# The output projection's operand splits, queued one by one behind the weight splits of the running pair

## The chip, the cores and the metric

The kernel runs on one core of one Trainium2 chip. The metric is the device time of one execution, in microseconds (us), from a launch to its end; lower is better. The engines are TensorE (PE in the rows), VectorE (DVE), ScalarE (ACT), GpSimd (POOL) and SyncE (SP), which here only issues DMAs. Each works its own queue in order and waits on semaphores for the others.

## What is computed

One layer of a hybrid decoder trunk on x of 1024 x 1024 float32: an RMSNorm, one combined input projection, three causal token mixers beside each other (differential attention a, sliding-window attention b, forgetting attention c), a gate and an up-projection for each, a merge by sigmoid gates, an output projection with w_o, a residual add and a last RMSNorm.

```
h = rms_norm(x, norm_gain[l], RMS_EPS)
proj = jnp.einsum('bsd,de->bse', h, w_in[l])
...
merged = gates[:, :, 0] * ua + gates[:, :, 1] * ub + gates[:, :, 2] * uc
x = x + jnp.einsum('bsd,de->bse', merged, w_o[l])
...
return rms_norm(x, final_gain, RMS_EPS)
```

## The kernel before

A float32 product is made of three matmuls on a reduced float32 type: each operand is split into a high half (a cast, `hi`) and a low half (the source less the high half, `lo`), and `mm3` (L106) adds hi x hi, hi x lo and lo x hi in PSUM for each block of 128 rows of the contraction. `split` (L98) makes the two halves: with `act` set the cast runs on ACT (L101), and the subtraction runs on POOL (L104). `operand` (L145) splits a weight tile of 128 x 512 elements into `w_hi` and `w_lo`, which have four buffers each (`NW`); so a weight cast waits until PE has read the buffer's tile of four operands earlier.

The stages follow each other: the norm and the v columns; then the pair stage of this change; then attention with fillers on PE; then the up-projections; then the output projection.

The pair stage (the loop over `tiles`, two by two) makes 40 column tiles of the input projection for q, k and the gates. Two tiles at a time go through `strassen` (L158), which turns the 2 x 2 block product into 7 products instead of 8, each of 12 matmuls of 512 columns. Its weight operands are, in the order in which PE takes them: a11, s2, a12, s3, s1, s4, a22. Those with s are sums and differences of the four weight tiles, made on DVE by `comb` (L165, tile `w_sf`); the others are the loaded tiles (`w_st`, five buffers). In code, a11, a12 and s2 are split before the first result is yielded, s3 and s1 before the second, s4 before the third and a22 before the last. A result is scaled and split (`qk_hi`, `qk_lo`) or made a gate (`sg`) and stored to DRAM by SP.

The output projection at the kernel's end is a Strassen product too, and its seven w_o operands are made during the pair stage by `prepare` (L456). For each of four blocks k it loads four tiles of w_o (`ws`, four buffers; the load is ordered behind the last w_st load), takes four differences of them on DVE (L471, L472, L478, L481) and calls `put` (L447) seven times. A put casts its source on ACT to `pwh`, subtracts on POOL to `pwl` (both from one ring of `NPW` = 3 buffers) and stores both halves to the DRAM tensor `wod` through SP. From the second pair on, the loop takes one step of `prepare` at the first and at the second result of each pair: 8 steps a block, one of them the loads, 28 puts in all.

The order on each engine isn't that of the code. A scheduler arranges the instructions from their dependencies and a simulated timeline, and takes what it holds ready; nothing ties the puts to a place but their sources and buffers. `tc.issue_after(ins)` adds such a tie: instructions in its block that run on the engine of `ins` are queued behind it there. It is an order and no semaphore.

Of the kernel before, what the change touches and what calls it, by code (L numbers as in the profile page):

```python
# [9 lines left out]
F32 = mybir.dt.float32  # L10
F32R = mybir.dt.float32r
AF = mybir.ActivationFunctionType
ALU = mybir.AluOpType
# [7 lines left out]
NB = S // P  # L21
# [14 lines left out]
LAG, AHEAD, TVLAG = 2, 3, 1  # L36
# [13 lines left out]
def hybrid_block_kernel(ctx, tc, x, norm_gain, w_in, b_forget, lambda_q1, lambda_k1, lambda_q2, lambda_k2,  # L50
                        subln_gain, sinks, w_up_a, w_up_b, w_up_c, w_o, final_gain, out):
    nc = tc.nc
    x = x[0]
    out = out[0]
# [43 lines left out]
    def split(src, hi, lo, act=False, eng=nc.gpsimd):  # L98

        if act:  # L100
            nc.scalar.copy(hi, src)  # L101
        else:
            nc.gpsimd.tensor_scalar(out=hi, in0=src, scalar1=1.0, scalar2=1.0, op0=ALU.mult, op1=ALU.mult)
        return eng.tensor_tensor(lo, src, hi.bitcast(F32), ALU.subtract)  # L104

    def mm3(ps, w, r, start=True, stop=True, n=4):  # L106

# [26 lines left out]

    behind = [None]

    def load_st(src):
        st = wp.tile([P, 4, P], F32, name="w_st", bufs=NST)
        behind[0] = nc.sync.dma_start(st, src)
        return st  # L140

    def load_half(col0, i):
        return load_st(w_in[:, 4 * i:4 * i + 4, col0:col0 + P])

    def operand(st, act=False):  # L145
        wh = wp.tile([P, 4, P], F32R, name="w_hi", bufs=NW)
        wl = wp.tile([P, 4, P], F32R, name="w_lo", bufs=NW)
        split(st, wh, wl, act)
        return wh, wl

    def direct_tile(col0, psum, act=False):
# [64 lines left out]
    with tc.tile_pool(name="blk", bufs=8) as blk, \  # L216
# [6 lines left out]
        with tc.tile_pool(name="xp", bufs=2) as xp:  # L223

            last = {}
# [56 lines left out]
            def load_vw(ch, dma=nc.sync):  # L282

                n = 392 if ch == 0 else 384
                w = []
                if ch == 0:
                    fc = xp.tile([P, 8, 8], F32, name="fc", bufs=1)
                for i in range(2):
                    wh = blk.tile([P, 4, n], F32R, name=f"vw_h{ch}{i}", tag="blk", padded_shape=[P, 4, 512])
                    wl = blk.tile([P, 4, n], F32R, name=f"vw_l{ch}{i}", tag="blk", padded_shape=[P, 4, 512])  # L290
                    (c0, n0), (c1, n1) = v_cols[ch]
                    for k0, nk, o, c, cn in ((0, 4, 0, c0, n0), (0, 2, n0, c1, n1), (2, 2, n0, c1, n1)):
                        ws = wp.tile([P, nk, cn], F32, name=f"vw_s{ch}", tag="w_st", bufs=NST)
                        dma.dma_start(ws, w_in[:, 4 * i + k0:4 * i + k0 + nk, c:c + cn])
                        last["lo"] = split(ws, wh[:, k0:k0 + nk, o:o + cn], wl[:, k0:k0 + nk, o:o + cn], True)
                    w.append((wh, wl))
                if ch == 0:
                    nc.sync.dma_start(fc, w_in[:, :, FC:FC + 8])
                    for i in range(2):
                        split(fc[:, 4 * i:4 * i + 4, :], w[i][0][:, :, 384:392], w[i][1][:, :, 384:392], True)  # L300
                return w, n
# [114 lines left out]
        with tc.tile_pool(name="qkp", bufs=2, reuse_waits="tile") as qkp:  # L416
# [32 lines left out]
            def put(dst, k, src):  # L449

                hi, lo = (qkp.tile([P, 512], F32R, name=f"pw{t}", tag="pw", bufs=NPW) for t in "hl")
                split(src, hi, lo, True)
                for t, v in enumerate((hi, lo)):
                    nc.sync.dma_start(dst[t, :, k, :], v.bitcast(F32))

# [42 lines left out]
            for n in range(0, len(tiles), 2):  # L498
                first = ExitStack()
# [41 lines left out]
    def gate_tiles(br):  # L541
        yg[br] = [[hp_.tile([P, 4, 512], F32R, name=f"yg_{br}{c}{t}", tag="h", bufs=8) for t in range(2)]
                  for c in range(2)]
# [29 lines left out]
    with tc.tile_pool(name="at", bufs=2, reuse_waits="tile") as at, \  # L573
# [14 lines left out]
        def fill(n):  # L588
            owed[0] += n
            while owed[0] >= 1:  # L590
                owed[0] -= 1
                if left[0] > cur["keep"]:
                    left[0] -= 1
                    next(filler)
# [11 lines left out]
        def load_q(row, m):  # L606
            return load_rows(row, m, (0, 1))

        def load_k(row, m):
            return [load_rows(row, m, (t, t)) for t in range(2)]  # L610

        def load_v(unit):

            v = at.tile([P, NB, 2 * P], F32R, name="v")
            nc.sync.dma_start(v.bitcast(F32), vd[:, unit, :].rearrange("(kb p) e -> p kb e", p=P))
            return v
# [254 lines left out]
        def load_b(u, kv):  # L871
            if kv == 0:
                vb["v"] = load_v(0)
            r = slice(20 * P + 64 * kv, 20 * P + 64 * kv + 64)
            u["k"] = []
            for t in range(2):
                tg = ("e", NE) if kv and t else ("f", NF)
                k = at.tile([P, S], F32R, name=f"kb{kv}{t}", tag=tg[0], bufs=tg[1])
                for d in range(2):
                    nc.sync.dma_start(k[64 * d:64 * d + 64, :].bitcast(F32), qd[t, r, :])  # L880
                u["k"].append(k)
            u["q"] = [load_q(16 + 2 * kv + t, m) for t in range(2) for m in range(2)]
# [3 lines left out]
        def load_c(u, hp, hh):  # L886
            if hh == 0:
                vc[hp] = load_v(1 + hp)
            u["v"] = vc[hp]
            u["q"] = load_q(hp, hh)  # L890
            u["k"] = load_k(4 + hp, hh)

        def load_a(u, h):
            u["v"] = load_v(5 + h)
            u["q"], u["k"] = [None, None], [None, None]
            for m in range(2):
                u["q"][m] = load_q(8 + h, m)
                u["k"][m] = load_k(12 + h, m)

        parts = []  # L900
        for kv in range(2):
            u = {}
            parts += [((lambda u=u, kv=kv: load_b(u, kv)) if i == 0 else None, "b", part_b(u, kv, i)) for i in range(NB)]
        for hp in range(4):
            for hh in range(2):
                u = {}
                parts += [((lambda u=u, hp=hp, hh=hh: load_c(u, hp, hh)) if g == 3 else None, "c", part_c(u, hp, hh, g))
                          for g in (3, 2, 1, 0)]
        for h in range(4):
            u = {}  # L910
            parts += [((lambda u=u, h=h: load_a(u, h)) if g == 3 else None, "a", part_a(u, h, g)) for g in (3, 2, 1, 0)]

        rate = {"b": FILL_B, "c": FILL_C, "a": FILL_A}
        pending_v = []
        ahead = 0
# [8 lines left out]
        def tick(c):  # L924
            clock[0] += c
            for e in list(later):
                if e[0] <= clock[0]:
                    later.remove(e)
                    e[1]()
        gq = [gb[0][0]] + [f for n in range(8) for f in ([gb[n + 1][0]] if n < 7 else []) + [gb[n][1]]]  # L930
        for n in range(len(parts) + LAG):
            if "free" in cur:
                if "b" not in yg:
                    gate_tiles("b")
                for f in gq[:GPART]:
                    f()
                del gq[:GPART]

            while ahead < min(n + AHEAD + 1, len(parts)):
                if parts[ahead][0]:  # L940
                    parts[ahead][0]()
                if ahead >= len(parts):
                    break
                ahead += 1
            if n == 0:
                fill(FILL_0)
                parts[0][2][3]()
            if n + 1 < len(parts):
                parts[n + 1][2][3]()
            sa = list(parts[n][2][0]) if n < len(parts) else []  # L950
            tv = []
            if n >= LAG:
                _, ta, va, _ = parts[n - LAG][2]
                for t, v in zip(ta, va):
                    tv.append(t)
                    pending_v.append(v)
                    if len(pending_v) > TVLAG:
                        tv.append(pending_v.pop(0))
            if n == len(parts) + LAG - 1:
                tv += pending_v  # L960
            kind = parts[min(n, len(parts) - 1)][1]
            cs, ct = sum(c for c, _ in sa), sum(c for c, _ in tv)
            ps_, pt_ = 0.0, 0.0
            while sa or tv:
                if sa and (not tv or (ps_ + 0.5 * sa[0][0]) * ct <= (pt_ + 0.5 * tv[0][0]) * cs):
                    c, f = sa.pop(0)
                    ps_ += c
                else:
                    c, f = tv.pop(0)
                    pt_ += c  # L970
                f()
                if n < len(parts):
                    fill(c * rate[kind] / 0.65)
                else:
                    cur["keep"] = 0
                    fill(c * FILL_Z / 0.65)
                tick(c * (1 + rate[kind]))
# [4 lines left out]
    with tc.tile_pool(name="st", bufs=2, reuse_waits="tile") as st, \  # L982
# [90 lines left out]
        for br, nxt in ("bc", "ca", "a "):  # L1073
            if nxt != " ":
                gate_tiles(nxt)
            for d in range(NK):
                n = UPS.index((br, d))
# [11 lines left out]
        for sb in range(NB // 2):  # L1089
# [8 lines left out]
            for j, c, u in strassen(*halves, wo, psum3,  # L1098
# [4 lines left out]
                if (j, c) != (1, 0):  # L1103
                    nc.vector.tensor_tensor(t, u, t, ALU.add)
                    u, t = t, u
# [40 lines left out]
```

## Time and profile before

| what | us |
|---|---|
| median of 3 runs (lowest, highest) | 1203.62 (1195.36, 1210.67) |
| the profiled execution, device time | 1201.41 |
| its span, first to last instruction | 1199.3 |
| busy in the span: PE | 1155.8 |
| DVE | 798.9 |
| POOL | 688.9 |
| ACT | 591.9 |

The mean granted clock of TensorE is 0.984 of its upper level. The device time holds 2.1 us outside of the span. Busy shares are averages over stages with different limits, and a matmul's row is longer than its share of PE, since matmuls overlap in it: the pace of PE is read from start to start.

### The profile page before, as it was taken

What the parts mean: (1) busy time and instruction counts of PE and PEld (TensorE: products, weight loads), DVE (VectorE), ACT (ScalarE), POOL (GpSimd) and SP (SyncE); (2) the same over time, 40 slices, a digit from 0 to 9 for tenths busy, and PEclk for the clock granted to TensorE, in tenths of its full rate; (3) what the DMA queues carried; (4) which work ended last, traced back from release to release, by engine and by line L of the source; (5) the groups of instructions that cost most, each with busy time, mean ns of one, the idle gap of its engine ahead of it and who ended that gap; (6) DMA issues with size and microseconds to landing.
All of it is one profiled execution on the core that took longest, in us unless ns stands there. A gap on an engine that the chain in (4) does not pass through costs nothing. (4 is left out here: it accounts for less than half of the span.)

```text
span 1199.3 us, 18793 instructions
## 1 busy us (share of the span) xinstructions
PE 1155.8 (96%) x5787; PEld 977.3 (81%) x5787; DVE 798.9 (67%) x1655; ACT 591.9 (49%) x1255; POOL 688.9 (57%) x684
## 2 busy tenths in 40 slices
PE   7999999999999999999999999999998999989997
PEld 6999878878778788887888888888877778878885
DVE  7667786766775774321887766767766835564897
ACT  6432334333443443332886666667876842334433
POOL 5056585665754754454555666665767632377652
PEclk8999999999999999999999999999999999999999
DMA  7442386675854643338945465456567359897332
GB/s 242 159 154 80 112 283 201 216 246 158 257 192 138 221 132 106 114 97 244 272 131 173 145 195 176 130 174 174 171 209 221 122 169 325 270 333 299 141 119 92
DMA packets 184531, 221.70 MB, mean 185 GB/s; under 512 B 16280, under 2 KB 116712, under 8 KB 182640
## 3 DMA queue, kind: packets, MB, share of 16 engines
q1 hardware_dynamic: 184288, 219.99, 58.2%
q8 instruction: 46, 0.75, 0.3%
q10 hardware_dynamic: 144, 0.52, 0.1%
q14 instruction: 53, 0.43, 0.1%
HBM read 144.89 MB, written 75.56 MB: 184 GB/s over the span
## 5 line engine op out<-in xcount | busy, mean ns | idle before, releaser
L104 POOL TENSOR_TENSOR w_lo<-w_st,w_hi 128x512 fp32r<-128x512 f32 x130 | 175.4, 1352 | 109.5 <-ACT w_hi L101 99.0
L104 POOL TENSOR_TENSOR w_lo<-w_sf,w_hi 128x512 fp32r<-128x512 f32 x96 | 137.8, 1440 | 107.4 <-ACT w_hi L101 100.6
L111 PE MATMUL pm<-t,w_lo 128*128 128x512 f32 x320 | 128.7, 402 | 5.4 <-POOL w_lo L104 5.4
L109 PE MATMUL pm<-t,w_hi 128*128 128x512 f32 x320 | 128.5, 402 | 2.5 <-ACT w_hi L101 2.5
L110 PE MATMUL pm<-t,w_hi 128*128 128x512 f32 x320 | 127.6, 399 | 0.0
L625 PE MATMUL sc<-qk 128*128 128x512 f32 (+2 forms) x384 | 102.4, 358 | 4.4 <-DVE m L645 3.8
L101 ACT CAST w_hi<-w_sf 128x512 fp32r<-128x512 f32 x96 | 58.9, 616 | 57.5 <-PE pm L110 51.4
L678 DVE TENSOR_TENSOR pt<-tp,pt 128x512 fp32r<-128x512 f32 x102 | 70.1, 687 | 23.5 <-ACT pt L677 22.7
L101 ACT CAST w_hi<-w_st 128x512 fp32r<-128x512 f32 x86 | 52.4, 617 | 62.0 <-PE pm L110 51.1
L111 PEld LDWEIGHTS pm<-t,w_lo 128*128 128x128 f32 x320 | 61.2, 191 | 21.5 <-POOL w_lo L104 7.1
L625 PEld LDWEIGHTS sc<-qk 128*128 128x128 f32 x384 | 64.9, 190 | 16.3 <-DVE m L645 6.8
L109 PEld LDWEIGHTS pm<-t,w_hi 128*128 128x128 f32 x320 | 61.2, 191 | 17.7 <-ACT w_hi L101 3.7
L110 PEld LDWEIGHTS pm<-t,w_hi 128*128 128x128 f32 x320 | 61.4, 192 | 14.5
L677 ACT CAST pt<-tp 128x512 fp32r<-128x512 f32 x102 | 59.4, 583 | 20.1 <-PE tp L671 18.8
L167 DVE TENSOR_TENSOR w_sf<-w_st 128x512 f32<-128x512 f32 x40 | 43.7, 1093 | 36.0 <-DMA w_st<-in_w_in_dram 21.8
L659 POOL TENSOR_SCALAR e_c<-e_c,r 128x1024 f32<-128x1024 f32 (+3 forms) x64 | 47.9, 748 | 24.5 <-DVE r L653 20.1
L651 ACT ACTIVATE e_c<-e_c,m 128x1024 f32<-128x1024 f32 (+3 forms) x64 | 49.9, 780 | 16.0 <-DVE m L645 15.1
L704 PE MATMUL y<-pt,v 128*128 128x256 f32 x336 | 55.4, 290 | 2.1 <-DVE pt L678 1.8
L651 ACT ACTIVATE e_a<-e_a,m 128x896 f32<-128x896 f32 (+7 forms) x64 | 49.6, 776 | 14.9 <-DVE m L645 14.4
L835 POOL TENSOR_TENSOR e_a<-e_a,e_a 128x896 f32<-128x896 f32 (+7 forms) x32 | 47.6, 1490 | 15.3 <-ACT e_a L834 15.1
L704 PEld LDWEIGHTS y<-pt,v 128*128 128x128 f32 x336 | 48.0, 189 | 6.8 <-DVE pt L678 3.2
L104 POOL TENSOR_TENSOR pwl<-ws,pwh 128x512 fp32r<-128x512 f32 x28 | 40.7, 1455 | 19.9 <-ACT pwh L101 14.2
(299 smaller groups left out, 3467.5 us busy)
## 6 DMA issues: line engine op xcount, KB each, us to landing
w_st<-in_w_in_dram SPq DMA_DIRECT2D x126, 256.0 KB, 3.3
qk<-qd SPq DMA_DIRECT2D x224, 128.0 KB, 3.0
wo<-wod SPq DMA_DIRECT2D x14, 1024.0 KB, 9.3
row<-gmd SPq DMA_DIRECT2D x48, 256.0 KB, 5.1
qd<-qk_hi SPq DMA_DIRECT2D x42, 256.0 KB, 4.2
qd<-qk_lo SPq DMA_DIRECT2D x42, 256.0 KB, 3.8
vd<-vt SPq DMA_DIRECT2D x24, 384.0 KB, 2.3
v<-vd SPq DMA_DIRECT2D x9, 1024.0 KB, 8.2
```

What stands on the lines that cost most here:

```text
L101: nc.scalar.copy(hi, src)
L104: return eng.tensor_tensor(lo, src, hi.bitcast(F32), ALU.subtract)
L109: nc.tensor.matmul(ps, w[0][:, k, :], r[0][:, k, :], start=start and k == 0, stop=False)
L110: nc.tensor.matmul(ps, w[0][:, k, :], r[1][:, k, :], start=False, stop=False)
L111: nc.tensor.matmul(ps, w[1][:, k, :], r[0][:, k, :], start=False, stop=stop and k == n - 1)
L625: nc.tensor.matmul(ps[:, :n], q, kk[t][c][:, o:o + n], start=t == 0, stop=t == 1)
L651: nc.scalar.activation(e[:, :L], e[:, :L], AF.Exp, bias=m2, scale=-1.0, accum_out=den)
L659: nc.gpsimd.tensor_scalar(out=e, in0=e, scalar1=r, scalar2=1.0, op0=ALU.mult, op1=ALU.mult)
L677: nc.scalar.copy(pt[:, 0, a:], tp[:, a:])
L678: nc.vector.tensor_tensor(pt[:, 1, a:], tp[:, a:], pt[:, 0, a:].bitcast(F32), ALU.subtract)
L704: nc.tensor.matmul(y[:, :256], l_, r_, start=t == 0 and n == 0, stop=last and n == len(mms) - 1)
L835: nc.gpsimd.tensor_tensor(e1[:, :L], e1[:, :L], e2[:, :L], ALU.add)
```

## The change

The cast and the subtraction of a put, until now made by `split`, are written out in `put`, and each is ordered behind its counterpart of the weight operand that was split last in the code before it: the cast behind that operand's cast on ACT, the subtraction behind its subtraction on POOL. For this, `split` returns both instructions and `operand` keeps them in `parts`. (A list that was called `parts` in the attention stage is renamed `units`, which is left out here.)

```diff
     def split(src, hi, lo, act=False, eng=nc.gpsimd):

         if act:
-            nc.scalar.copy(hi, src)
+            first = nc.scalar.copy(hi, src)
         else:
-            nc.gpsimd.tensor_scalar(out=hi, in0=src, scalar1=1.0, scalar2=1.0, op0=ALU.mult, op1=ALU.mult)
-        return eng.tensor_tensor(lo, src, hi.bitcast(F32), ALU.subtract)
+            first = nc.gpsimd.tensor_scalar(out=hi, in0=src, scalar1=1.0, scalar2=1.0, op0=ALU.mult, op1=ALU.mult)
+        return first, eng.tensor_tensor(lo, src, hi.bitcast(F32), ALU.subtract)
...
+    parts = [None, None]
...
     def operand(st, act=False):
         wh = wp.tile([P, 4, P], F32R, name="w_hi", bufs=NW)
         wl = wp.tile([P, 4, P], F32R, name="w_lo", bufs=NW)
-        split(st, wh, wl, act)
+        parts[:] = split(st, wh, wl, act)
         return wh, wl
...
             def put(dst, k, src):

                 hi, lo = (qkp.tile([P, 512], F32R, name=f"pw{t}", tag="pw", bufs=NPW) for t in "hl")
-                split(src, hi, lo, True)
+                with tc.issue_after(parts[0].ins):
+                    nc.scalar.copy(hi, src)
+                with tc.issue_after(parts[1].ins):
+                    nc.gpsimd.tensor_tensor(lo, src, hi.bitcast(F32), ALU.subtract)
                 for t, v in enumerate((hi, lo)):
                     nc.sync.dma_start(dst[t, :, k, :], v.bitcast(F32))
```

The first place is POOL's queue at the first puts. Operands of the first pair are w_lo_1490 to w_lo_1598 (1574 is its s4, 1598 its a22), those of the second begin with w_lo_1630 (a11); 1661 is its s2, 1727 its s1. Before:

```order
L104 TENSOR_TENSOR w_lo_1548<-w_sf_1476,w_hi_1547 128x512
L104 TENSOR_TENSOR pwl_1751<-ws_1698,pwh_1750 128x512
L104 TENSOR_TENSOR w_lo_1574<-w_sf_1482,w_hi_1573 128x512
L104 TENSOR_TENSOR w_lo_1598<-w_st_1455,w_hi_1597 128x512
L104 TENSOR_TENSOR pwl_1886<-ws_1702,pwh_1885 128x512
L104 TENSOR_TENSOR w_lo_1630<-w_st_1620,w_hi_1629 128x512
L104 TENSOR_TENSOR pwl_1936<-ws_1704,pwh_1935 128x512
L104 TENSOR_TENSOR w_lo_1656<-w_st_1622,w_hi_1655 128x512
L104 TENSOR_TENSOR pwl_2069<-ws_1698,pwh_2068 128x512
L104 TENSOR_TENSOR w_lo_1661<-w_sf_1649,w_hi_1660 128x512
L104 TENSOR_TENSOR pwl_2120<-ws_1700,pwh_2119 128x512
L104 TENSOR_TENSOR w_lo_1708<-w_sf_1651,w_hi_1707 128x512
```

The same queue now, from the second pair's s1 to the third pair's s4:

```order
L104 TENSOR_TENSOR w_lo_1727<-w_sf_1647,w_hi_1726 128x512
L457 TENSOR_TENSOR pwl_1751<-ws_1698,pwh_1750 128x512
L104 TENSOR_TENSOR w_lo_1759<-w_sf_1653,w_hi_1758 128x512
L104 TENSOR_TENSOR w_lo_1783<-w_st_1626,w_hi_1782 128x512
L104 TENSOR_TENSOR w_lo_1815<-w_st_1805,w_hi_1814 128x512
L104 TENSOR_TENSOR w_lo_1841<-w_st_1807,w_hi_1840 128x512
L104 TENSOR_TENSOR w_lo_1846<-w_sf_1834,w_hi_1845 128x512
L457 TENSOR_TENSOR pwl_1886<-ws_1702,pwh_1885 128x512
L104 TENSOR_TENSOR w_lo_1893<-w_sf_1836,w_hi_1892 128x512
L104 TENSOR_TENSOR w_lo_1912<-w_sf_1832,w_hi_1911 128x512
L457 TENSOR_TENSOR pwl_1936<-ws_1704,pwh_1935 128x512
L104 TENSOR_TENSOR w_lo_1944<-w_sf_1838,w_hi_1943 128x512
```

The first put (pwl_1751) has moved from the first pair's s4 to behind the second pair's s1, and the next two stand behind s2 and s1 of the third pair, where five puts stood among seven weights. This goes on at two puts a pair.

The second place is ACT's queue at the same puts. Before:

```order
L101 CAST pwh_1750<-ws_1698 128x512
L101 CAST w_hi_1573<-w_sf_1482 128x512
L101 CAST pwh_1885<-ws_1702 128x512
L101 CAST w_hi_1597<-w_st_1455 128x512
L101 CAST w_hi_1629<-w_st_1620 128x512
L421 ACTIVATE qk_hi_1521<-u_1474 128x512
L101 CAST pwh_1935<-ws_1704 128x512
L101 CAST w_hi_1655<-w_st_1622 128x512
L101 CAST pwh_2068<-ws_1698 128x512
L421 ACTIVATE qk_hi_1565<-u_1563 128x512
```

And now, around the puts behind s2 (w_hi_1845) and s1 (w_hi_1911) of the third pair:

```order
L101 CAST w_hi_1845<-w_sf_1834 128x512
L455 CAST pwh_1885<-ws_1702 128x512
L423 ACTIVATE qk_hi_1775<-u_1676 128x512
L101 CAST w_hi_1892<-w_sf_1836 128x512
L423 ACTIVATE qk_hi_1799<-u_1723 128x512
L101 CAST w_hi_1911<-w_sf_1832 128x512
L455 CAST pwh_1935<-ws_1704 128x512
L174 COPY u_1830<-pm_1813 128x512
L101 CAST w_hi_1943<-w_sf_1838 128x512
```

A put's cast now has two to three weight casts between it and the next, where two followed each other with one weight cast between them. PE's queue is the same but for two places where two matmuls of a12's product stand a few rows later; the stages behind the pair stage are the same on all engines.

## Rows read from the trace of the kernel before

**Rows 1.** The page, part 1: busy time of each engine.

```profile
PE 1155.8 (96%) x5787; PEld 977.3 (81%) x5787; DVE 798.9 (67%) x1655; ACT 591.9 (49%) x1255; POOL 688.9 (57%) x684
```

**Rows 2.** Busy time by stretch: stretch, length, busy us (x instructions) by engine, PEclk, DMA.

```profile
190.00:230.00 40.00, 40.00 (x175) 32.52 (x174) 26.91 (x34) 17.70 (x30) 22.03 (x16) 1.00 0.63 201
...
470.00:510.00 40.00, 40.00 (x175) 32.52 (x174) 15.53 (x23) 14.77 (x25) 18.59 (x15) 1.00 0.38 106
```

**Rows 3.** Waits of PE from 150 to 430 us: total, times, longest.

```profile
PE pm L111 <- POOL w_lo L104: 5.4, 4, 2.3
PE pm L109 <- ACT w_hi L101: 1.8, 2, 0.9
```

**Rows 4.** Timeline of PE at four places: start us, us, instruction, [idle before <-releaser].

```profile
164.28 0.40 PE L109 MATMUL pm<-h10h,w_hi 128*128 128x512 f32 x1
167.00 0.62 PE L111 MATMUL pm<-t,w_lo 128*128 128x512 f32 x1 [2.32 <-POOL w_lo L104]
...
170.75 0.39 PE L111 MATMUL pm<-t,w_lo 128*128 128x512 f32 x1
...
245.31 0.39 PE L111 MATMUL pm<-h00h,w_lo 128*128 128x512 f32 x1
...
249.16 0.80 PE L111 MATMUL pm<-t,w_lo 128*128 128x512 f32 x1 [1.15 <-POOL w_lo L104]
...
252.67 0.39 PE L110 MATMUL pm<-t,w_hi 128*128 128x512 f32 x1
...
327.00 0.39 PE L111 MATMUL pm<-h00h,w_lo 128*128 128x512 f32 x1
...
334.60 0.39 PE L111 MATMUL pm<-t,w_lo 128*128 128x512 f32 x1
...
409.40 0.40 PE L109 MATMUL pm<-h10h,w_hi 128*128 128x512 f32 x1
410.56 0.50 PE L111 MATMUL pm<-t,w_lo 128*128 128x512 f32 x1 [0.76 <-POOL w_lo L104]
410.89 0.39 PE L109 MATMUL pm<-t,w_hi 128*128 128x512 f32 x1
```

**Rows 5.** Busy time by stretch, around the first of these places.

```profile
164.00:171.00 7.00, 4.68 (x14) 3.34 (x14) 6.26 (x7) 1.71 (x4) 5.51 (x4) 0.76 1.00 327
```

**Rows 6.** Timeline of POOL at the first of these places.

```profile
163.90 1.38 POOL L104 TENSOR_TENSOR pwl<-ws,pwh 128x512 fp32r<-128x512 f32 x1 [0.30 <-PE pm L110]
165.24 1.71 POOL L104 TENSOR_TENSOR w_lo<-w_sf,w_hi 128x512 fp32r<-128x512 f32 x1
```

**Rows 7.** What ended ACT's idle time before the puts' casts: us, times.

```profile
  DMA ws<-in_w_o_dram: 13.0, 6
...
  DMA wod<-pwl: 9.3, 7
```

**Rows 8.** Timeline of POOL in a pair without puts: s2, s3, s1, s4.

```profile
463.33 1.29 POOL L104 TENSOR_TENSOR w_lo<-w_sf,w_hi 128x512 fp32r<-128x512 f32 x1 [1.46 <-ACT w_hi L101]
466.12 1.30 POOL L104 TENSOR_TENSOR w_lo<-w_sf,w_hi 128x512 fp32r<-128x512 f32 x1 [1.50 <-ACT w_hi L101]
468.86 1.29 POOL L104 TENSOR_TENSOR w_lo<-w_sf,w_hi 128x512 fp32r<-128x512 f32 x1 [1.44 <-ACT w_hi L101]
471.86 1.30 POOL L104 TENSOR_TENSOR w_lo<-w_sf,w_hi 128x512 fp32r<-128x512 f32 x1 [1.71 <-ACT w_hi L101]
```

**Rows 9.** Timeline of PE in that pair: first matmul of s3's and s4's product.

```profile
473.68 0.40 PE L109 MATMUL pm<-t,w_hi 128*128 128x512 f32 x1
...
479.27 0.39 PE L109 MATMUL pm<-h11h,w_hi 128*128 128x512 f32 x1
```

**Rows 10.** The puts' subtractions by tile: ns min/median/max, first and last start; landing.

```profile
L104 POOL TENSOR_TENSOR pwl<-ws,pwh x28: 1280/1306/1832, 152.1 to 411.0; 128x512 fp32r<-128x512 f32 x28
...
DMA to landing us min/median/max: 2.8/3.8/5.0
```

**Rows 11.** DVE's subtractions on w_o tiles, one of four lines.

```profile
L471 DVE TENSOR_TENSOR ws<-ws x4: 675/1774/1783, 154.0 to 391.6; 128x512 f32<-128x512 f32 x4
```

More of the change, by code (lines that the diff above doesn't have):

```diff
@@ L294, in load_vw @@
                         dma.dma_start(ws, w_in[:, 4 * i + k0:4 * i + k0 + nk, c:c + cn])
-                        last["lo"] = split(ws, wh[:, k0:k0 + nk, o:o + cn], wl[:, k0:k0 + nk, o:o + cn], True)
+                        last["lo"] = split(ws, wh[:, k0:k0 + nk, o:o + cn], wl[:, k0:k0 + nk, o:o + cn], True)[1]
                     w.append((wh, wl))
@@ L898, in load_a @@
                 u["k"][m] = load_k(12 + h, m)
-        parts = []
+        units = []
         for kv in range(2):
             u = {}
-            parts += [((lambda u=u, kv=kv: load_b(u, kv)) if i == 0 else None, "b", part_b(u, kv, i)) for i in range(NB)]
+            units += [((lambda u=u, kv=kv: load_b(u, kv)) if i == 0 else None, "b", part_b(u, kv, i)) for i in range(NB)]
         for hp in range(4):
@@ L906, in hybrid_block_kernel @@
                 u = {}
-                parts += [((lambda u=u, hp=hp, hh=hh: load_c(u, hp, hh)) if g == 3 else None, "c", part_c(u, hp, hh, g))
+                units += [((lambda u=u, hp=hp, hh=hh: load_c(u, hp, hh)) if g == 3 else None, "c", part_c(u, hp, hh, g))
                           for g in (3, 2, 1, 0)]
@@ L910, in hybrid_block_kernel @@
             u = {}
-            parts += [((lambda u=u, h=h: load_a(u, h)) if g == 3 else None, "a", part_a(u, h, g)) for g in (3, 2, 1, 0)]
+            units += [((lambda u=u, h=h: load_a(u, h)) if g == 3 else None, "a", part_a(u, h, g)) for g in (3, 2, 1, 0)]
         rate = {"b": FILL_B, "c": FILL_C, "a": FILL_A}
@@ L930, in hybrid_block_kernel @@
         gq = [gb[0][0]] + [f for n in range(8) for f in ([gb[n + 1][0]] if n < 7 else []) + [gb[n][1]]]
-        for n in range(len(parts) + LAG):
+        for n in range(len(units) + LAG):
             if "free" in cur:
@@ L937, in hybrid_block_kernel @@
                 del gq[:GPART]
[L939 to L942, printed above, removed]
+            while ahead < min(n + AHEAD + 1, len(units)):
+                if units[ahead][0]:
+                    units[ahead][0]()
+                if ahead >= len(units):
                     break
@@ L946, in hybrid_block_kernel @@
                 fill(FILL_0)
[L947 to L950, printed above, removed]
+                units[0][2][3]()
+            if n + 1 < len(units):
+                units[n + 1][2][3]()
+            sa = list(units[n][2][0]) if n < len(units) else []
             tv = []
             if n >= LAG:
-                _, ta, va, _ = parts[n - LAG][2]
+                _, ta, va, _ = units[n - LAG][2]
                 for t, v in zip(ta, va):
@@ L958, in hybrid_block_kernel @@
                         tv.append(pending_v.pop(0))
-            if n == len(parts) + LAG - 1:
+            if n == len(units) + LAG - 1:
                 tv += pending_v
-            kind = parts[min(n, len(parts) - 1)][1]
+            kind = units[min(n, len(units) - 1)][1]
             cs, ct = sum(c for c, _ in sa), sum(c for c, _ in tv)
@@ L971, in hybrid_block_kernel @@
                 f()
-                if n < len(parts):
+                if n < len(units):
                     fill(c * rate[kind] / 0.65)
```

## The prediction

> **What bounds the kernel now.** I read the page first. TensorE (PE) is busy 1155.8 of the span's 1199.3 us [rows 1], so a change pays only where PE stands still or runs slower than it can. The change touches the stage that makes the q, k and gate tiles in pairs, roughly 140 to 515 us, so the second view is the busy time by stretch in that stage. In two stretches without any put of the output projection (190 to 230 and 470 to 510) PE is busy 40.00 of 40.00 us at a granted clock of 1.00, that is at the upper of its two levels, 2.4 GHz, and issues 175 matmuls [rows 2]: 40 / 175 = 0.229 us from start to start. Nothing can be gained there: while PE is fed, its own work is the bound. So I looked for where it isn't fed. The waits of PE between 150 and 430 us are six: four for w_lo (the subtraction on POOL, 5.4 us) and two for w_hi (the cast on ACT, 1.8 us) [rows 3]. Both are halves of the weight split, so PE starves for operands. No wait for a DMA, a PSUM buffer or DVE is in that list.
>
> The third view, PE's starts in order of time, tells what each place costs, as I count the time from the last matmul at the normal pace to the first one at it again, and take off 0.229 us for each start that lies in it [rows 4]:
> - 164.28 to 170.75: 6.47 us for 10 starts, 6.47 - 2.29 = 4.18 us
> - 245.31 to 252.67: 7.36 us for 14 starts, 7.36 - 3.21 = 4.15 us
> - 327.00 to 334.60: 7.60 us for 15 starts, 7.60 - 3.44 = 4.16 us
> - 409.40 to 410.89: 1.49 us for 2 starts, 1.49 - 0.46 = 1.03 us
>
> The sum is 13.5 us. Only 7.2 of it is idle time [rows 3]; the other 6.3 us is that PE restarts at the lower level, 1.2 GHz, after the first three of these places: in the stretch around the first one the mean granted clock is 0.76 [rows 5]. The fourth place (a wait of 0.76 us) brings no slow stretch [rows 4].
>
> The fourth view says why it starves at just these four places. All 28 puts (7 for each of the four k blocks) stand in four bunches, and the losses lie in them. At the first loss POOL runs a put's subtraction from 163.90 (1.38 us) and only behind it, with no idle time between, the w_lo for which PE has stopped: it ends at 165.24 + 1.71 = 166.95, and PE goes on at 167.00 [rows 6]. ACT is held in the bunches too: before the casts of the puts it stood idle 13.0 us for w_o tiles that hadn't landed and 9.3 us for the store that frees a buffer of the put's ring of three [rows 7]; every weight cast behind such a cast waits as well.
>
> **The change, part by part.** It adds no instruction and takes none away: 28 casts, 28 subtractions, 56 stores, 16 loads and 16 DVE subtractions as before. Three things move.
>
> First, the casts and subtractions. The put of a product is now queued behind the split of the operand that was traced last before it: s2 for the first put of a pair, s1 for the second. The order shows one subtraction behind s2's w_lo and one behind s1's in each pair, instead of up to seven spread through three pairs' weights. A pair is 7 products of 12 matmuls, 84 x 0.229 = 19.2 us, so two puts come in 19.2 us. I take the place behind s1 as the hardest, as s4's split stands directly behind it. In the clean stretch s4's w_lo starts at 471.86 after 1.71 us of idle POOL, ends at 473.16, and PE begins s4's product at 479.27: a lead of 6.1 us. For s3, behind the other put, it is 473.68 - 467.42 = 6.3 us [rows 8, 9]. A put's subtraction takes 1.28 to 1.83 us, median 1.31 [rows 10]; at its longest, with none of it in POOL's idle time, 6.1 - 1.83 = 4.3 us of lead stay. On ACT the cast is shorter than that (it feeds the subtraction). What hides both is thus the lead of three products that the four w_hi and w_lo buffers give; cost on PE: 0. If that cover were gone, each put would cost up to a place like the first three, 4.2 us.
>
> One page bears on this. By the rows a subtraction on POOL is at most 1.83 us beside DVE's work [rows 10]. The Trainium skill, SBUF — State Buffer, section "Who interferes with whom", has it that a VectorE instruction with two SBUF inputs and a GpSimd instruction that reads SBUF exclude each other for a whole instruction. DVE's longest subtraction on w_o tiles is 1.78 us [rows 11], so by that rule a put could be 1.83 + 1.78 = 3.6 us on POOL. The lead would shrink to 2.5 us and the sum would not change, but rival D would be nearer.
>
> Second, the stores, and the loads of the next block. SP works its queue in order, and each wod store now stands two per pair among the loads of w_st and the stores of qd. A store waits for the put, and the w_st loads behind it wait too. In the bunches up to six put stores stood between two weight loads; now it is at most three. The ring has three buffers for the two halves of a put, so the cast half of a pair's first put must be stored before the second put's subtraction. Their places on POOL lie as far apart as the splits of s2 and s1, 463.33 to 468.86, 5.5 us [rows 8], and a store lands 3.8 us after it is issued (median; 5.0 at most) [rows 10]. So of the 9.3 us of waits for the ring [rows 7] little should be left, and a rest of 1 or 2 us stays inside the lead of 4.3 us. The w_o loads of block k + 1 go out as the tiles of block k come free, the first two some 20 us before their put. I cost these at 0, hidden by that distance. The trace of before has no paced put; the bounds from its rows are 0 from below (a stretch of pairs without puts loses nothing, so a paced one can't do better) and from above the 13.5 us that the bunches lose now. I take 1.0 us, the size of the mildest place (1.03), as the clean stretches are the nearer row: PE stalls there not once.
>
> Third, DVE's 16 subtractions on w_o tiles come in pairs ahead of s4's combination. DVE is busy 15.5 to 26.9 of 40 us in the clean stretches [rows 2]; two of at most 1.78 us [rows 11] fit, and s4 is needed a whole pair later.
>
> The later stages keep their orders on all engines, and none is tied to an absolute time: what the stage saves goes through to the end.
>
> Sum: 1201.41 - 13.5 + 1.0 = 1188.9 us for the profiled execution (its span of 1199.3 and 2.1 around it). That execution is 2.2 us under the median of the runs, 1203.62, so for a median I say 1203.62 - 12.5 = 1191.1 us, 1.0% less.
>
> **The rivals.**
> B: half goes. At the head of each block the put's cast still waits on ACT for its w_o tile, as now (13.0 us in 6 waits, [rows 7]), and with it the next weight casts. For: the loads of a block start only when its predecessor is nearly done. Against: the put that reads the first tile is a pair away from the load. With half of the 13.5 us left: 1203.6 - 6.7 = 1196.9 us.
> C: nothing goes. The same POOL and ACT work is there, and PE starves in other places: 1203.6 us. That would be so if POOL were short of time, not order. Against: in the clean stretches POOL is busy 18.6 to 22.0 of 40 us [rows 2]; two puts a pair add 2 x 1.31 x 40 / 19.2 = 5.5 us.
> D: slower. The put is now fixed in ACT's and POOL's order: if its source or buffer is late by more than the lead, s4's cast waits behind it in every pair. That decides from a wait of 6.1 - 1.83 = 4.3 us on a put, and the longest single wait that now stands before one on ACT is of that order (13.0 us in 6, [rows 7]). One such wait a pair in 14 pairs costs 14 x 4.18 = 58.5 us: 1203.6 - 13.5 + 58.5 = 1248.6 us. Nine of them would do for 2% (9 x 4.18 - 13.5 = 24.1). Against: those waits came from seven puts sharing three buffers in a bunch.
>
> **How the numbers follow.** My forecast (12.5 us less) gets 0.72, B 0.16, C 0.08, D 0.04. The gain can't pass the 13.5 us that are lost, 1.1%, so faster by over 2%, about what a measurement of this kernel can tell from no change, needs runs that scatter: the three of before lie from 1195.36 to 1210.67. I give it 0.04, slower by over 2% 0.03 (most of D), within 2% 0.93. For the range: below, 1191.1 less some 8 us of that scatter, 1183; above, C's 1203.6, which takes in B: 1183 to 1204.
>
> **What would show it.** Right: no wait of PE for w_lo or w_hi from 150 to 460 us, or few under 1 us; granted clock 1.00 in every slice there; the puts' subtractions two per 19.2 us up to about 460 us instead of 411; waits for the put's buffers gone. The end of the pair stage then comes about 12.5 us earlier and all after it is shifted by as much. Wrong: casts of puts that wait for w_o tiles with PE stalled behind them (B), gaps of PE in most pairs (C), or a clock at 1.2 GHz that comes back pair after pair (D).

## The result and the profile after

The changed kernel takes 1188.43 us (median of 4 runs, 1186.46 to 1194.19), the kernel before 1205.36 us (median of 4, 1195.36 to 1210.67). The ratio is 0.9897, with a 95% interval of 0.9859 to 0.9935: faster by 1.0%, and inside 2%. (The quotient of the two medians is 0.986; the four runs after scatter by 8 us, those before by 15.) The profiled execution took 1188.05 us with a span of 1186.2 us, 13.4 and 13.1 us less than before.

The pair stage is where this comes from. Part 1 of the profile's page, as [rows 1], says of the kernel after:

```profile
PE 1149.9 (97%) x5787; PEld 973.9 (82%) x5787; DVE 807.1 (68%) x1655; ACT 588.2 (50%) x1255; POOL 692.8 (58%) x684
```

and the busy time by stretch, with the columns of [rows 2], of the part of the stage with puts:

```profile
140.00:460.00 320.00, 319.33 (x1384) 259.33 (x1383) 237.91 (x268) 131.11 (x230) 210.24 (x145) 1.00 0.63 202
```

PE has as many instructions as before, and over 320 us with all 28 puts in them it stands still for 0.7 us, at a granted clock of 1.00. Its waits, which were six and 7.2 us between 150 and 430 us [rows 3], are one between 140 and 520 us:

```profile
PE pm L109 <- ACT w_hi L101: 0.7, 1, 0.7
```

This one lies at 143 us, ahead of the first put, in both kernels. The clearest reading is the start of each pair on PE, the first matmul of a11's product. Before, the second, third and last pair start at

```profile
161.06 0.40 PE L109 MATMUL pm<-h00h,w_hi 128*128 128x512 f32 x1
...
184.60 0.39 PE L109 MATMUL pm<-h00h,w_hi 128*128 128x512 f32 x1
...
523.60 0.39 PE L109 MATMUL pm<-h00h,w_hi 128*128 128x512 f32 x1
```

and after at

```profile
161.13 0.39 PE L109 MATMUL pm<-h00h,w_hi 128*128 128x512 f32 x1
...
180.53 0.39 PE L109 MATMUL pm<-h00h,w_hi 128*128 128x512 f32 x1
...
510.33 0.39 PE L109 MATMUL pm<-h00h,w_hi 128*128 128x512 f32 x1
```

After, each of the 18 distances from the second pair's start to the last one's is 19.40 us, 349.2 in all. Before, the pairs without puts had 19.40 too, and the four in which PE starved had 23.54, 23.49, 23.51 and 20.40. So I call the loss of the stage what lies between those two starts over 349.2 us: 362.54 - 349.2 = 13.34 us before, 349.20 - 349.2 = 0.00 after. The experiments below are read by this number: there is one trace of each kernel, pairs without puts take 19.4 us in all of them, and the whole time scatters by more than what is looked for.

On POOL and ACT the puts wait for nothing any more: before the casts and subtractions of puts (rows of before: [rows 7]) the tile views of the kernel after list no idle time of ACT or POOL at all. The subtractions' own row is

```profile
L457 POOL TENSOR_TENSOR pwl<-ws,pwh x28: 1287/1524/1755, 167.9 to 457.3; 128x512 fp32r<-128x512 f32 x28
```

so they go on to 457 us where they ended at 411 [rows 10], and one takes 1.52 us in the median instead of 1.31. On ACT, as on POOL, two or five weight splits stand between two puts, seven at a block's end; the two to three that the section on the change gives for ACT are too few.

### The profile page after: what moved, and what is told of

Same layout as the page of the kernel before. It is cut to its first block, busy times and chain, and to the rows that moved or that the text cites. A ratio compares the mean times of both kernels' runs of the same rounds, so it can differ in the third digit from the quotient of the medians.

```text
span 1186.2 us, 18774 instructions
## 1 busy us (share of the span) xinstructions
PE 1149.9 (97%) x5787; PEld 973.9 (82%) x5787; DVE 807.1 (68%) x1655; ACT 588.2 (50%) x1255; POOL 692.8 (58%) x684
## 5 line engine op out<-in xcount | busy, mean ns | idle before, releaser
L104 POOL TENSOR_TENSOR w_lo<-w_sf,w_hi 128x512 fp32r<-128x512 f32 x96 | 143.1, 1493 | 98.2 <-ACT w_hi L101 91.5
L109 PE MATMUL pm<-t,w_hi 128*128 128x512 f32 x320 | 126.3, 395 | 0.7 <-ACT w_hi L101 0.7
L111 PE MATMUL pm<-t,w_lo 128*128 128x512 f32 x320 | 126.3, 395 | 0.0
L110 PE MATMUL pm<-t,w_hi 128*128 128x512 f32 x320 | 126.0, 394 | 0.0
L169 DVE TENSOR_TENSOR w_sf<-w_st 128x512 f32<-128x512 f32 x40 | 49.6, 1240 | 40.1 <-DMA w_st<-in_w_in_dram 28.7
L109 PEld LDWEIGHTS pm<-t,w_hi 128*128 128x128 f32 x320 | 60.1, 188 | 14.9 <-ACT w_hi L101 1.1
L110 PEld LDWEIGHTS pm<-t,w_hi 128*128 128x128 f32 x320 | 60.1, 188 | 14.2
L423 ACT ACTIVATE qk_hi<-u 128x512 fp32r<-128x512 f32 x32 | 20.3, 633 | 91.0 <-DVE u L191 42.7
```

The lines of the kernel that those rows point to most:

```text
L104: return first, eng.tensor_tensor(lo, src, hi.bitcast(F32), ALU.subtract)
L109: nc.tensor.matmul(ps, w[0][:, k, :], r[0][:, k, :], start=start and k == 0, stop=False)
L110: nc.tensor.matmul(ps, w[0][:, k, :], r[1][:, k, :], start=False, stop=False)
L111: nc.tensor.matmul(ps, w[1][:, k, :], r[0][:, k, :], start=False, stop=stop and k == n - 1)
L169: nc.vector.tensor_tensor(t, x, y, op)
```

## The experiments

My theory: PE starved since the scheduler packed seven puts into each bunch, so that POOL's and ACT's queues could not keep the weight splits ahead of PE; the ties cure it by spreading them. The rivals for the cause are the ring of three buffers, the w_o loads that hold ACT, the place among the operands instead of the pace, and the two ties, of which perhaps one does it all.

**One tie alone.** First only the cast's tie is kept:

```diff
                 with tc.issue_after(parts[0].ins):
                     nc.scalar.copy(hi, src)
-                with tc.issue_after(parts[1].ins):
-                    nc.gpsimd.tensor_tensor(lo, src, hi.bitcast(F32), ALU.subtract)
+                nc.gpsimd.tensor_tensor(lo, src, hi.bitcast(F32), ALU.subtract)
```

> Only the casts of the puts are tied (on ACT); their subtractions are free on POOL. If the pace of the puts is what counts, one tie is enough, since a subtraction can't come before its cast: all pairs 19.4 us apart on PE, none of the 13.3 us that the kernel before loses in the pair stage, ratio to it 0.990 as for the change. If the tie on POOL does a part of the work, subtractions bunch again and the stage loses at least 3 us, ratio above 0.992.

Measured: loss of the stage 0.00 us, ratio 0.9905 (0.9873 to 0.9937). The order of all instructions on POOL and on ACT is that of the change, so this is the change once more. The other half alone:

```diff
-                with tc.issue_after(parts[0].ins):
-                    nc.scalar.copy(hi, src)
+                nc.scalar.copy(hi, src)
```

> Only the subtractions are tied (on POOL); the casts are free on ACT. If the pace counts, the ring of three buffers holds the casts to the pace of the subtractions, and PE loses at most 1 us in the pair stage, ratio 0.990. If a cast that runs ahead blocks ACT (it then waits there for a buffer of the ring), weight casts wait behind it and PE loses 4 us or more, ratio 0.993 or above.

Measured: loss 0.00 us, ratio 0.9892 (0.9848 to 0.9935). Some casts run a pair ahead here, and one of them held ACT for 6.2 us while its w_o tile landed; PE didn't notice. Either tie is enough, and the second adds nothing.

**What starves PE in a bunch.** The kernel before, with the puts' subtractions on DVE:

```diff
-                split(src, hi, lo, True)
+                split(src, hi, lo, True, nc.vector)
```

> The kernel before, bunches and all, with the puts' subtractions on DVE instead of POOL. If POOL's time in the bunches starves PE, its waits for w_lo go away and the pair stage loses under 4 us in place of 13.3, ratio about 0.992. If it is ACT, held before the puts' casts by w_o tiles and the ring, the waits of PE stay (for w_hi now) and the loss is 8 us or more, ratio 0.996 or above.

Measured: ratio 0.9952 (0.9928 to 0.9977), nearer to that of the second answer; the loss is that of the first. It falls from 13.34 to 3.54 us; the pair before the first measured one is 1.2 us longer (32.44 us to its successor, 31.23 before). PE's waits from 150 to 430 us:

```profile
PE pm L111 <- POOL w_lo L104: 1.7, 2, 0.9
PE pm L109 <- DVE u L186: 1.0, 1, 1.0
PE pm L109 <- ACT w_hi L101: 0.8, 1, 0.8
```

So the puts on POOL are the larger part. ACT is held before their casts as long as before (12.0 us for w_o tiles and 16.4 us for stores; in the kernel before 13.0 and 9.3), and with POOL free of puts that costs PE little. This doesn't yet say that it is the time of the subtractions: what left POOL's queue with them is also what they wait for there. In the second bunch of the kernel before, a put's cast had held ACT, its subtraction then held POOL idle, and the w_lo for which PE waits 1.15 us stands right behind (ACT and POOL by time):

```profile
245.40 0.62 ACT L101 CAST pwh<-ws 128x512 fp32r<-128x512 f32 x1 [3.77 <-POOL w_lo L104]
246.15 1.28 POOL L104 TENSOR_TENSOR pwl<-ws,pwh 128x512 fp32r<-128x512 f32 x1 [1.13 <-DMA wod<-pwl]
247.39 1.72 POOL L104 TENSOR_TENSOR w_lo<-w_sf,w_hi 128x512 fp32r<-128x512 f32 x1
```

The third and the fourth bunch look the same, with POOL idle for 1.33 and 1.06 us at that place; in the first it had been idle for 0.30 us only [rows 6]. The kernel before with a larger ring:

```diff
-NPW, UPAHEAD, WARM = 3, 2, 14
+NPW, UPAHEAD, WARM = 5, 2, 14
```

> The kernel before with five buffers in the puts' ring instead of three. If waits for the ring starve PE, the loss in the pair stage falls from 13.3 to under 5 us, ratio 0.993 or below. If POOL's time in the bunches does it, the puts come even closer together and the loss stays at 10 us or more, ratio 0.997 to 1.005.

Measured: ratio 0.9999 (0.9978 to 1.0019), loss 10.80 us. The scheduler packs the puts closer now: between the first and the last put of a block stand four to six weight splits, where six to eight stood before. The loss is that of the second answer, but it adds up two effects. The second, third and fourth bunch lose less than before (pairs of 21.33, 20.77 and 20.00 us, in place of 23.49, 23.51 and 20.40): 3.9 us in all instead of 9.2. POOL is not idle directly before the puts and splits that PE waits for there. The first bunch loses more (26.30 in place of 23.54), with a wait of PE for one cast on ACT, the longest of the stage:

```profile
PE pm L109 <- ACT w_hi L101: 3.6, 1, 3.6
PE pm L111 <- POOL w_lo L104: 2.8, 4, 1.2
PE pm L109 <- DVE u L186: 0.2, 1, 0.2
```

That wait comes from DVE. The cast stands on ACT behind a result's cast (`qk_hi`), which waits 4.15 us for its `u`, and DVE's queue has two differences of w_o tiles directly before that `u`, which in the kernel before came behind it:

```profile
161.00 1.78 DVE L478 TENSOR_TENSOR ws<-ws 128x512 f32<-128x512 f32 x1
162.81 1.64 DVE L481 TENSOR_TENSOR ws<-ws 128x512 f32<-128x512 f32 x1
164.37 0.68 DVE L199 TENSOR_TENSOR u<-pm,u 128x512 f32<-128x512 f32 x1
165.08 0.63 ACT L421 ACTIVATE qk_hi<-u 128x512 fp32r<-128x512 f32 x1 [4.15 <-DVE u L199]
```

So the ring has a share in three of the four bunches, and a third engine's queue can starve PE by the same packing. Both at once, subtractions on DVE and five buffers:

> The kernel before with the puts' subtractions on DVE and five buffers in the ring, still bunched. Moved to DVE alone, 3.5 us of the 13.3 us were left (and the first pair was 1.2 us longer). If the ring makes up that rest, under 1 us stays in the pairs with puts; if it is the wait of ACT for w_o tiles that have not landed, 2 us or more stays, most of it in the first pair with puts.

Measured: loss 1.60 us, in two pairs (0.77 and 0.85), both by waits of PE for w_lo of 0.5 us and less; that is between the two answers. The stage's first pair takes 34.85 us, 3.6 us longer. With it 5.2 us are left, most of it in the first pair, as the second answer has it, and no less than the 4.7 us (3.54 and 1.2) with three buffers. Two things stand in that pair. A put's cast holds ACT's queue while its w_o tile lands, as in the kernel before:

```profile
152.09 0.62 ACT L101 CAST pwh<-ws 128x512 fp32r<-128x512 f32 x1 [5.81 <-DMA ws<-in_w_o_dram]
```

But PE's one long wait there (1.9 us) is for DVE, and DVE is busy all the time, with puts' subtractions and differences of w_o tiles (busy by stretch; DVE is the third engine, after PE and PEld):

```profile
158.00:166.00 8.00, 6.11 (x20) 4.62 (x19) 8.00 (x14) 3.42 (x6) 2.68 (x2) 0.79 0.81 244
```

So the landing of w_o, rival B's mechanism, holds ACT in a free order, but that it costs PE time is not shown.

**Place or pace.** If the ties only spread the puts, tied puts in a bunch should be as bad as free ones. With the ties kept, the steps are taken two at a time in two of every four pairs:

```diff
-                    if n >= 2 and j == c:
+                    if n >= 2 and j == c and (n // 2) % 4 in (1, 2):
+                        next(prep_, None)
                         next(prep_, None)
```

> The change with its ties, but the puts are bunched again by hand: two steps of the preparation at each result in the second and third of every four pairs, none in the other two, so 7 puts fall into two pairs (3 or 4 a pair; before, 7 in some two and a half). If the place behind s2 and s1 is what helps, where three operands' lead is at its full length, the pair stage loses under 3 us in all. If it is the pace, it loses as much as the kernel before, 10 us or more, ratio to it 0.998 or above.

Measured: loss 0.67 us, ratio 0.9932 (0.9909 to 0.9955). By the expectation's words the place would have won. But the premise was mis-sized: counted in the order, between the first and the last of a block's seven puts stand six to eight splits in the kernel before, about one pair and not two and a half, and nine or ten here. So I made it as dense as before, with the ties: four steps at each result of every fourth pair. (The ratio is not as good as the loss lets expect, 12.7 of 1199 us or 0.989; the stage is all that I read it for, and the rest stays open.)

```diff
-                    if n >= 2 and j == c:
-                        next(prep_, None)
+                    if n >= 2 and j == c and (n // 2) % 4 == 1:
+                        for _ in range(4):
+                            next(prep_, None)
```

> Tied as in the change, but four steps of the preparation at each result in one of every four pairs: 7 puts among some seven weight splits, as dense as in the kernel before (there 7 puts stand among seven or eight). If density is what starves PE (POOL has 7 splits and 7 subtractions in a pair, 7 x 1.5 + 7 x 1.5 = 21 us of 19.4, and the ring turns over more than four times), the stage loses 8 us or more. If being tied behind s2 and s1 is what helps, it loses under 3 us.

Measured: loss 9.09 us (time of its one run 1196.96, of the kernel before beside it 1204.24). Five or six splits stand between a block's first and last put. So the place alone doesn't do it. PE waits nearly as long as in the kernel before, for the same two tiles:

```profile
PE pm L111 <- POOL w_lo L104: 5.8, 5, 1.6
PE pm L109 <- ACT w_hi L101: 0.6, 2, 0.4
```

The same with five buffers in the ring:

> The one before with five buffers in the ring. If POOL's time in the dense pair is short, the loss stays within 30% of the run before; if the ring is what holds the splits back, it falls to a third or less, under 4 us.

Measured: loss 6.74 us, 74% of the run before, so POOL's time by the bound that was set. The trace doesn't bear this out as it stands, since the scheduler packs the puts closer again (four splits) and five buffers don't suffice for that: four of PE's five waits stand behind a put for which POOL had been idle 2.0 us, until the store that frees its buffer; that is longer than PE then waits (0.91 to 1.46 us). POOL's waits of this kind from 150 to 430 us:

```profile
POOL pwl L457 <- DMA wod<-pwl: 9.8, 5, 2.1
```

POOL's time is scarce as well. The groups of POOL's instructions from 242 to 267 us, where the second bunch lies (count, busy us, mean ns, idle time before them and what ended it); dense with five buffers:

```profile
L457 POOL TENSOR_TENSOR pwl<-ws,pwh 128x512 fp32r<-128x512 f32 x6 | 10.0, 1674 | 2.1 <-DMA wod<-pwl 2.1
L104 POOL TENSOR_TENSOR w_lo<-w_sf,w_hi 128x512 fp32r<-128x512 f32 x5 | 8.2, 1654 | 0.0
L104 POOL TENSOR_TENSOR w_lo<-w_st,w_hi 128x512 fp32r<-128x512 f32 x3 | 4.3, 1446 | 0.0
```

and the changed kernel in the same stretch:

```profile
L104 POOL TENSOR_TENSOR w_lo<-w_sf,w_hi 128x512 fp32r<-128x512 f32 x5 | 7.5, 1508 | 7.8 <-ACT w_hi L101 7.8
L457 POOL TENSOR_TENSOR pwl<-ws,pwh 128x512 fp32r<-128x512 f32 x3 | 4.8, 1593 | 0.0
L104 POOL TENSOR_TENSOR w_lo<-w_st,w_hi 128x512 fp32r<-128x512 f32 x3 | 4.3, 1445 | 3.0 <-ACT w_hi L101 3.0
```

In the dense pair no weight split finds POOL idle: it is busy 10.0 + 8.2 + 4.3 = 22.5 of 25 us and idle 2.1 more for the ring. In the changed kernel it has been idle 7.8 + 3.0 = 10.8 us before the splits, waiting for their casts: POOL has time left.

**How far the pace can go.** Two steps at every result without a pause, 7 puts in two pairs, done after eight pairs:

```diff
                     if n >= 2 and j == c:
                         next(prep_, None)
+                        next(prep_, None)
```

> The change, with two steps of the preparation at each result of a pair all the time: 7 puts in two pairs without a pause, done after eight pairs. POOL has 7 splits and 3.5 subtractions to do a pair, 7 x 1.4 + 3.5 x 1.5 = 15 us of 19.4, so its time suffices. If the lead hides the puts at this pace too, each pair stays at 19.4 us and nothing is lost; if the pace is what hurts, each of the eight pairs loses 1.7 us or more (what a bunch lost by the pair), 13 us in all, ratio 1.00.

Measured: loss 10.57 us, ratio 1.000 (0.9973 to 1.0026), in seven of eight pairs, nearly half of it (4.85 us) in one. POOL's timeline in that pair:

```profile
264.50 1.30 POOL L457 TENSOR_TENSOR pwl<-ws,pwh 128x512 fp32r<-128x512 f32 x1
270.47 1.26 POOL L457 TENSOR_TENSOR pwl<-ws,pwh 128x512 fp32r<-128x512 f32 x1 [4.67 <-ACT qk_hi L423]
```

A second subtraction behind the same split waits for 4.7 us while two more splits stand behind it. The profile puts the wait down to a cast of ACT that came last; that it is the ring was then tried with five buffers:

> The one before with five buffers in the puts' ring instead of three. If a second put behind the same operand waits for the ring and holds the split of the next operand back, the loss of the run before falls to under a third with this; if POOL's time is what is short, the loss stays within 30% of it (if there is none in the run before, none here).

Measured: loss 0.84 us, a twelfth. At 3.5 puts a pair POOL's time is enough, and three buffers aren't.

**How much lead is needed.** The change with three buffers each for w_hi and w_lo:

```diff
-NST, NW, NSF = 5, 4, 4
+NST, NW, NSF = 5, 3, 4
```

> The change with three buffers each for w_hi and w_lo instead of four: an operand can be split only two products ahead, so the lead of s4's split falls by one product, from 6.1 to some 3.3 us. A put's subtraction (1.3 to 1.8 us) still fits into that, so pairs with puts should not be longer than the last three without by more than 0.3 us each; if a put's whole stay of 2.4 us (cast and subtraction) plus POOL's own 1.3 us must be hidden, they are 0.5 us or more longer each, 7 us over the stage. The other stages use these buffers too, so only the pair stage is read.

Measured: all pairs 19.37 to 19.39 us from the second on, with and without puts, and no wait of PE. (The stage's first pair takes 32.33 instead of 31.2 us.) A lead of two products covers a paced put as well as three do.

The change and all that lose something in one table (either tie alone and the run with three buffers for weights lose nothing). Splits are the weight splits between the first and the last put of a block, in the order in which they and the puts' subtractions start; waits are those of PE in the stage (without the one at 143 us):

| puts | splits | ring | waits, us | loss, us |
|---|---|---|---|---|
| free (before) | 6 to 8 | 3 | 7.2 | 13.34 |
| free | 4 to 6 | 5 | 6.6 | 10.80 |
| tied, dense | 5 to 6 | 3 | 6.4 | 9.09 |
| tied, dense | 4 | 5 | 4.9 | 6.74 |
| tied, twice, no pause | 10 | 3 | 6.9 | 10.57 |
| tied, twice, no pause | 9 | 5 | 0.3 | 0.84 |
| tied, bunch and pause | 9 to 10 | 3 | 0.3 | 0.67 |
| tied, one at a result (the change) | 21 | 3 | 0 | 0.00 |
| free, subtractions on DVE | 5 to 8 | 3 | 3.5 | 3.54 |
| free, subtractions on DVE | 4 to 5 | 5 | 2.8 | 1.60 |

(In the last two rows part of the waits lies in the stage's first pair, which the loss doesn't count: it takes 1.2 and 3.6 us longer.) What the loss holds beyond the waits is lost around them: in the kernel before most of it where the clock falls, in the two dense runs none of it, as the granted clock is 1.00 around each of their bunches.

No version beats the change: its pair stage has no loss left that the puts cause.

## Why the prediction was right

**The loss of 13.5 us and its places.** Right, to 0.2 us: by the starts of pairs it is 13.34. The half that is no waiting (6.3 us, most of it at the lower clock) went with the waits, as the granted clock of 1.00 over 320 us shows.

**What is left, 1.0 us.** Mis-sized, by the whole of it: nothing is left. The better row was the one that I named as the nearer one, the clean pairs. The gain of the profiled execution was 13.4 us where 12.5 were forecast; by the ratio it is 0.0103 x 1205.4 = 12.4 us. The medians, 1188.43 where 1191.1 was forecast, lie 16.9 us apart, more than the stage lost; four runs that scatter by 15 us don't carry that difference.

**The lead that hides a put.** Right that it does, wrong in its size. I took 6.1 us less a subtraction, 4.3 us. POOL's timeline in a pair with two puts (s1's split, the put, s4's split) and the start of s4's product on PE:

```profile
361.39 1.29 POOL L104 TENSOR_TENSOR w_lo<-w_sf,w_hi 128x512 fp32r<-128x512 f32 x1 [2.40 <-ACT w_hi L101]
362.64 1.74 POOL L457 TENSOR_TENSOR pwl<-ws,pwh 128x512 fp32r<-128x512 f32 x1
364.34 1.74 POOL L104 TENSOR_TENSOR w_lo<-w_sf,w_hi 128x512 fp32r<-128x512 f32 x1
```

```profile
369.01 0.39 PE L109 MATMUL pm<-h11h,w_hi 128*128 128x512 f32 x1
```

The split ends at 364.34 + 1.74 = 366.08, 2.9 us ahead; the smallest such lead in the stage is 2.1 us. I took it that the put takes none of POOL's idle time, and it takes all that it needs: from s1's split to s4's it is 2.95 us here and 3.00 us in the pair without puts [rows 8], where POOL was idle in between. What I left out is that s4's split itself is slower here (1.74 against 1.30 us, [rows 8]), and that s1's split starts late, 7.6 us before s4's product instead of 10.4 [rows 8, 9]: POOL had been idle 2.40 us for its cast. That the cover is the lead of three products wasn't right either: with three buffers, a lead of two, no pair lost anything. What covers a put is that POOL has the time for it within the pair.

**The rule on the port shared by DVE and POOL** (the Trainium skill, SBUF — State Buffer, "Who interferes with whom") would, by the prediction's estimate, have allowed a put 3.6 us on POOL. The longest took 1.755 us, so the row was the better guide to the size. In the changed kernel's pair stage those of POOL's subtractions that met no DVE work on two SBUF tiles took 1.3 us, and all that took 1.67 us or more lay beside 0.6 us or more of such work. That fits with a shared port; no run here changes DVE's work alone.

**The ring and the w_o loads.** Right: no put waits for either. I had left 1 or 2 us to the ring; it is 0. At twice the pace the ring is what loses (10.57 against 0.84 us with five buffers), so that margin isn't wide. My reading of [rows 7] was incomplete: its second line holds 2.6 us of idle time of POOL (before casts on ACT it is 6.7 us for stores of pwl and 2.6 us for stores of pwh), and three waits of casts, 12.0 us in all, which the view puts down to POOL's splits, are left out of it.

**The rivals.** B (half goes) and C (nothing goes) fell: no wait for a w_o tile stands before a put, and POOL, at 1.5 us for a put, had the time. D (slower) didn't come, but its mechanism was seen at twice the pace: a put that waits 4.7 us for its ring with splits queued behind it.

**The cause of the bunches' loss.** The order's density is what the runs show: with four to eight splits between a block's first and last put and the subtractions on POOL, PE waits 4.9 to 7.2 us, whether the puts are free or tied; with nine or more it waits 0.3 us or not at all where the ring turns over in time. By what path a dense order costs PE time differs from place to place. Of the 13.34 us most comes through the puts on POOL (3.54 are left, and 1.2 added elsewhere, with the subtractions on DVE), but that is their time and their waits for the ring together: with five buffers three bunches lose 3.9 us instead of 9.2. DVE's differences of w_o tiles cost time where they are packed, too. How much of the 13.34 us is each one's stays open; I had it too simple when I set POOL's time against the ring.

## What to carry to other kernels

Work that no one waits for can still starve the engine that counts, if a scheduler is free to pack it in front of work that is waited for on an in-order queue: count how many such pieces stand among how many urgent ones in the order, and compare the time of both, their waits for buffers included, with the time that the bounding engine takes for the urgent ones. Tie it behind something that comes at a steady pace; one tie at the head of its chain is enough. Then size its buffers by the distance of two pieces at that pace against the landing time of a store.

## What the runs showed of the hardware

The lower clock does not follow from the length of idle time alone. Before, two waits of 0.89 and 1.15 us that lay 2.6 us apart were followed by some 3 us at the lower level, 1.2 GHz; PE's timeline in the second bunch, where the starts go from 0.23 us apart (246.93 to 247.16) to 0.43 (249.75 to 250.18), behind the second wait, which ends at 249.16 [rows 4]:

```profile
246.59 0.50 PE L109 MATMUL pm<-t,w_hi 128*128 128x512 f32 x1 [0.89 <-ACT w_hi L101]
246.93 0.40 PE L110 MATMUL pm<-t,w_hi 128*128 128x512 f32 x1
247.16 0.39 PE L109 MATMUL pm<-h10h,w_hi 128*128 128x512 f32 x1
...
249.75 0.63 PE L109 MATMUL pm<-t,w_hi 128*128 128x512 f32 x1
250.18 0.63 PE L110 MATMUL pm<-t,w_hi 128*128 128x512 f32 x1
```

In the tied dense run three waits of PE from 180 to 187 us (1.63, 0.37 and 1.04 us) cost no clock, as the granted clock of the stretch around them shows:

```profile
175.00:190.00 15.00, 11.96 (x50) 8.83 (x49) 8.59 (x11) 5.59 (x10) 10.30 (x8) 1.00 0.84 276
```

So 2.0 us of waits made a pair 4.1 us longer in the one kernel, and 3.0 us of waits made one 3.9 us longer in the other. What tells the two apart was not tried.
